# The state product of a chunked SSD scan as three products of split operands, with the state updated in place

## The chip, the cores and the metric

The kernel runs on one core of one Trainium2 chip. The metric is device time in microseconds of one execution. The kernel before took 1280.56 us, the median of three runs (1280.24 to 1281.42).

## The reference, cut to what matters

One decoder layer: a gated pooling branch beside a Mamba-2 state space branch, for a prompt of 1024 positions and for 8 short samples. The part that matters is the scan of the prompt. It goes over chunks of 128 positions; there are 32 heads of 64 channels in 4 groups, a state of 128 x 64 per head, and B and C are shared by the 8 heads of a group:

```python
def step(h, inp):
    xq, dq, Bq, Cq = inp
    acs = jnp.cumsum(dq * Ag, axis=1)
    ...
    y = jnp.einsum('bijge,bjgep->bigep', att, xq)
    y = y + jnp.einsum('bign,bige,bgepn->bigep', Cq, jnp.exp(acs), h)
    last = acs[:, -1]
    w_in = jnp.exp(last[:, None] - acs) * dq
    h = h * jnp.exp(last)[..., None, None] + jnp.einsum('bjgn,bjge,bjgep->bgepn', Bq, w_in, xq)
    return h, y
```

The last line but one is the state's update: the old state decayed, plus the product of B with x weighted by w_in. The change is about this line. All tensors are float32.

## The kernel before, in words

The kernel first normalises x, multiplies it with the input weights, and stores the branches' inputs in DRAM. Then comes a stretch in which TensorE (PE) alternates between two kinds of work, and in this stretch the change lies. At the end come the last group's output products, the product with w_o and the final norm.

**Two kinds of work.** One kind is 32 chunk rows, `seq`, each made by the generator `chunk(g, c)` for group g and chunk c. The other kind is blocks of output products (`gemm_`, L353 to L364, from `P_unit` and `S_unit`): 12 matmuls into one of three PSUM buffers (`psA`), in fp32r, a form of float32 in which the kernel multiplies split operands, a high half and a low half, as three products (L359 to L361). Such a block's result is taken from PSUM by ScalarE (ACT, L1741) or VectorE (DVE, L1723, L1744).

**The steps of a chunk row** are the stretches between the `yield` lines of `chunk`:

1. Loads by SP of the decays, B and C, and x (L1491 to L1497). x has five buffers, `xb`.
2. For c > 0 the factor cE of C, an exponential on ACT (L1501); the mask on GpSimd (POOL, L1192, called by `far`); eight exponentials on ACT (L1201, called by `exps`).
3. PE transposes x into the PSUM tile px and B into pbc, and multiplies B with C into pbc (L1510 to L1513). ACT copies B to `bt` (L1515) and C into pbc (L1517). DVE makes xd = x times dt (L1521) and xw = x times the weight (L1523, one buffer), and multiplies dec and cE with what stands in pbc (L1528, L1530).
4. The state product of bt and xw, a float32 matmul, into the single buffer of `psC` (L1535). Then `inner`: 16 products of xd and dec (L1213) and of the old state and cE (L1216) by head, in tiles of 64 columns. POOL decays the old state into a second buffer (L1541), DVE adds the product (L1543). DVE combines x and the inner products, four instructions (L1548), in place in x's buffer.
5. `finish` (L1468 to L1479): gate, split of the result, sum of squares. In the last chunk of a group a sixth step transposes the state (L1555) and stores it.

px, pbc and the result of `inner` take turns in the four PSUM buffers of `psB`.

**What sets the order.** A loop over i (L1807 to L1826) calls the steps of several rows in turn: step 3 of row i+1, some blocks of products, step 4 of row i, loads (step 1) of row i+3, step 2 of row i+2, step 5 of row i, more blocks. From i = 13 on, the split of w_o runs beside (`wo_splits`: ACT L1778, POOL L1780). PE and SP run the instructions in just the written order (`ORDER`, `in_line`). ACT, DVE and POOL each run their own in an order that a planner of the framework sets when the kernel is built, from its own costs and from the written order as the priority; on the chip each engine then works strictly in that order. Before the loop comes a prelude (L1799 to L1804) whose order is fixed on PE, ACT, DVE and SP.

Of the kernel before, what the change touches and what calls it, by code (L numbers as in the profile page):

```python
# [8 lines left out]
F32 = mybir.dt.float32  # L9
F32R = mybir.dt.float32r  # L10
AF = mybir.ActivationFunctionType
ALU = mybir.AluOpType
# [8 lines left out]
P = 128  # L21
# [25 lines left out]
def tile_pool_ssd_step(  # L47
# [6 lines left out]
    nc = tc.nc  # L54
    uid = [0]

    def nm(s):
        uid[0] += 1
        return f"{s}_{uid[0]}"
# [52 lines left out]
    mm = nc.tensor.matmul  # L112
    act = nc.scalar.activation
    V = nc.vector
# [1344 lines left out]
    hst = [None] * NG  # L1459
# [3 lines left out]
    def ckt(shape, tag, bufs=2):  # L1463
        return (cl if tag in CKL else ca if tag in ("dec", "xb", "cE", "bc") else ck).tile(list(shape), F32, tag=tag, name=nm(tag), bufs=bufs)
# [24 lines left out]
    def chunk(g, c):  # L1489
        o = c * P  # L1490
        dec = ckt([P, 8, P], "dec", 3)  # L1491
        decays(dec, g, c)
        bc = ckt([P, 2, P], "bc", 3)
        load(bc, xbc_d[g][:, 4:6, o:o + P])
        Bf, Cf = bc[:, 0], bc[:, 1]
        xb = ckt([P, 4, P], "xb", 5)
        load(xb, xbc_d[g][:, 0:4, o:o + P])  # L1497
        yield
        if c > 0:
            cE = ckt([P, 8, P], "cE")  # L1500
            act(cE, dec, AF.Exp, scale=-1.0)  # L1501
        if g > 0 or c > 0:
            far(dec, c)
            exps(dec, g, c)
            yield
        sz = ckt([P, 4, P], "sz", 3)
        load(sz, z_d[g][:, :, o:o + P])
        px = PB()
        for q in range(4):
            nc.tensor.transpose(px[:, q * P:(q + 1) * P], xb[:, q], ident)  # L1510
        pbc = PB()
        nc.tensor.transpose(pbc[:, :P], Bf, ident)
        mm(pbc[:, P:2 * P], Bf, Cf, start=True, stop=True)  # L1513
        bt = ckt([P, P], "bt", 2)
        act(bt, pbc[:, :P], AF.Copy)  # L1515
        if c > 0:
            act(pbc[:, 2 * P:3 * P], Cf, AF.Copy)  # L1517
        pxv = px.rearrange("p (h d) -> p h d", d=64)
        heads = slice(8 * g, 8 * g + 8)
        xd = ckt([P, 8, 64], "xd", 2)  # L1520
        V.tensor_tensor(xd, pxv, dtT[:, c, heads].unsqueeze(2).to_broadcast([P, 8, 64]), ALU.mult)  # L1521
        xw = ckt([P, 8, 64], "xw", 1)
        V.tensor_tensor(xw, pxv, wdT[:, c, heads].unsqueeze(2).to_broadcast([P, 8, 64]), ALU.mult)  # L1523
        if g == c == 0:
            yield
            far(dec, c)
            exps(dec, g, c)
        V.tensor_tensor(dec, dec, pbc[:, P:2 * P].unsqueeze(1).to_broadcast([P, 8, P]), ALU.mult)  # L1528
        if c > 0:
            V.tensor_tensor(cE, cE, pbc[:, 2 * P:3 * P].unsqueeze(1).to_broadcast([P, 8, P]), ALU.mult)  # L1530
        yield
        if c == 0:
            yh[g], yl[g] = [Y4(hs if g % 2 else hp) for _ in range(2)]
        pu = PC()
        mm(pu, bt, xw.rearrange("p h d -> p (h d)"), start=True, stop=True)  # L1535
        pi = inner(xd, dec, P, *((hst[g], cE) if c > 0 else ()))
        hn = ckt([P, 512], "hst", 2)
        if c == 0:
            act(hn, pu, AF.Copy)
        else:  # L1540
            nc.gpsimd.tensor_tensor(hn.rearrange("p (h d) -> p h d", d=64), hst[g].rearrange("p (h d) -> p h d", d=64),  # L1541
                                    Elb[:, c, heads].unsqueeze(2).to_broadcast([P, 8, 64]), ALU.mult)
            V.tensor_tensor(hn, hn, pu, ALU.add)  # L1543
        hst[g] = hn

        v = xb
        for q in range(4):
            V.scalar_tensor_tensor(v[:, q], v[:, q], Dv[:, 4 * g + q:4 * g + q + 1], pi[:, q], ALU.mult, ALU.add)  # L1548
        yield
        finish(g, o, P, v, sz)  # L1550
        if c == NC - 1:
            yield
            pt = PB()
            for q in range(4):
                nc.tensor.transpose(pt[:, q * P:(q + 1) * P], hn[:, q * P:(q + 1) * P], ident)  # L1555
            fo = ckt([P, 4, P], "xb", 5)
            act(fo, pt.rearrange("p (q n) -> p q n", n=P), AF.Copy)
            store_(new_ssm_p[0, 0, 8 * g:8 * g + 8].rearrange("(q h) p n -> (h p) q n", h=2), fo)
# [241 lines left out]
    for _ in range(FRONT - 1):  # L1800
        next(pc_)
    next(seq[0])
    next(seq[1])
    next(pc_)  # L1804
    in_line(first_engines)
    order = tuple(mybir.EngineType[e] for e in ORDER)
    for i in range(len(seq)):  # L1807
        if i + 1 < len(seq):
            next(seq[i + 1])
        products(i + 0.4)  # L1810
        if i > 0:
            next(seq[i - 1], None)
        next(seq[i], None)
        if i % NC == 2:
            ends = sample_end(i // NC)
            next(ends)
        if i + 3 < len(seq):
            next(seq[i + 3])
        if i + 2 < len(seq):
            next(seq[i + 2])  # L1820
        next(seq[i], None)
        if i % NC == 4:
            next(ends, None)
        if i > 12:
            next(wos, None)
        products(i + 1.0)  # L1826
# [229 lines left out]
```

## Time and profile before

| | |
|---|---|
| median of three runs | 1280.56 us (1280.24 to 1281.42) |
| profiled execution | 1284.38 us, span 1282.6 us |
| granted PE clock, mean | 0.996 |
| busy over the span | PE 98%, DVE 71%, ACT 51%, POOL 51% |
| first state product (L1535) | 830.8 us after the span's start |
| last state product | 1099.7 us |
| state products recorded | 64, two per call, mean 591 ns |

The span is what the profiler saw from the first to the last instruction; the execution's own time is 1.8 us longer. "PEld" rows are weight loads of PE, which overlap with its matmuls. In a row of instructions in order of time, the first number is the start in us, the second the duration, then the engine, the line, the operation and the tiles (output, arrow, inputs), the count, and in square brackets the idle time before with what ended it. The tiles ps and pc are PSUM buffers of psB and psC, and mm is one of psA. In the view of waits a row gives who waited for whom, the us in total, the number of times and the longest.

### The profile page before, as it was taken

How to read it: one execution, taken by the hardware profiler on the slowest of the kernel's cores; microseconds unless marked ns; L12 is line 12 of the kernel's file. 1: busy time of each engine (PE TensorE's matmuls, PEld its weight loads, DVE VectorE, ACT ScalarE, POOL GpSimd, SP SyncE). 2: the span in 40 equal slices, each digit the busy share in tenths (PEclk: the TensorE clock that was granted, in tenths of full speed). 3: DMA queues.
4: the chain of work that ended last, by engine and by line, in shares of the span. 5: the costliest groups of instructions: out<-in, count | busy, mean ns of one | idle time of the engine just before them, and what ended most of it. 6: DMA issues, size and time to landing. Idle time of an engine off the chain costs nothing.

```text
span 1282.6 us, 26320 instructions
## 1 busy us (share of the span) xinstructions
PE 1256.3 (98%) x9739; PEld 1170.9 (91%) x9739; DVE 911.9 (71%) x1635; ACT 654.9 (51%) x1508; POOL 653.9 (51%) x556
## 2 busy tenths in 40 slices
PE   7999999999999999999999999999999999999997
PEld 6779999989999999999999999989889889999786
DVE  4686678976989588676676765488667887579343
ACT  4665337465546645454655554655676756202111
POOL 1007659677868878555444444345666867300000
PEclk9999999999999999999999999999999999999999
DMA  9736354465456453444556564999779898675531
GB/s 331 243 119 215 123 165 154 152 208 171 143 164 212 152 161 124 165 154 121 171 173 197 170 187 147 331 306 305 231 221 278 271 295 266 211 265 180 212 107 50
DMA packets 232769, 251.68 MB, mean 196 GB/s; under 512 B 29729, under 2 KB 176881, under 8 KB 232634
## 3 DMA queue, kind: packets, MB, share of 16 engines
q1 hardware_dynamic: 160544, 171.60, 42.8%
q10 hardware_dynamic: 72098, 78.41, 17.8%
q8 instruction: 77, 1.26, 0.4%
q14 instruction: 50, 0.41, 0.1%
HBM read 167.06 MB, written 83.01 MB: 195 GB/s over the span
## 4 chain that ended last, share of the span: by engine, by line
PE 74%; issue 3%; DMA 2%; DVE 2%; POOL 2%; ACT 1%; ACTq 0%; SPq 0%; POOLq 0%; DVEq 0%
PE mm L359 7%; PE mm L360 6%; PE mm L361 6%; PE ps L608 6%; PE ps L609 6%; PE mm L608 6%; PE ps L610 6%; PE mm L610 6%; PE mm L609 6%; PE ps L1213 3%; PE ps L2002 2%; PE ps L2003 2%; PE ps L2004 2%; PE pc L1535 2%; PE ps L1216 2%
## 5 line engine op out<-in xcount | busy, mean ns | idle before, releaser
L168 POOL TENSOR_TENSOR wlo<-rawA,whi 128x512 fp32r<-128x512 f32 x120 | 180.3, 1506 | 169.5 <-ACT whi L165 90.1
L168 POOL TENSOR_TENSOR wlo<-raw,whi 128x512 fp32r<-128x512 f32 x92 | 148.7, 1623 | 124.0 <-ACT whi L165 111.2
L359 PE MATMUL mm<-Y,whi 128*128 128x352 f32 (+1 forms) x480 | 163.9, 342 | 0.0
L360 PE MATMUL mm<-Y,whi 128*128 128x352 f32 (+1 forms) x480 | 158.0, 329 | 0.3 <-DVE Y L1573 0.3
L361 PE MATMUL mm<-Y,wlo 128*128 128x352 f32 (+1 forms) x480 | 157.6, 328 | 0.0
L610 PE MATMUL mm<-Y,wlo 128*128 128x272 f32 x496 | 144.2, 291 | 4.5 <-POOL wlo L168 4.0
L608 PE MATMUL mm<-Y,whi 128*128 128x272 f32 x496 | 146.3, 295 | 0.6 <-DVE GA L624 0.5
L608 PE MATMUL ps<-Y,whi 128*128 128x272 f32 x496 | 143.6, 290 | 0.2 <-ACT o L1068 0.2
L609 PE MATMUL ps<-Y,whi 128*128 128x272 f32 x496 | 143.0, 288 | 0.0
L609 PE MATMUL mm<-Y,whi 128*128 128x272 f32 x496 | 142.6, 288 | 0.0
L610 PE MATMUL ps<-Y,wlo 128*128 128x272 f32 x496 | 142.6, 287 | 0.0
L1056 DVE SCALAR_TENSOR_TENSOR GA<-GA,cvT,GA 128x1112 f32<-128x1112 f32 x72 | 125.5, 1746 | 1.9 <-ACT GA L1053 1.8
L165 ACT ACTIVATE whi<-rawA 128x512 fp32r<-128x512 f32 x125 | 78.3, 627 | 92.7 <-PE ps L609 49.1
L165 ACT ACTIVATE whi<-raw 128x512 fp32r<-128x512 f32 x96 | 58.9, 627 | 108.0 <-DVE raw L554 51.0
L610 PEld LDWEIGHTS mm<-Y,wlo 128*128 128x128 f32 x496 | 93.4, 188 | 6.5 <-POOL wlo L168 5.4
L1201 ACT ACTIVATE dec<-dec,acT 128x128 f32<-128x128 f32 (+1 forms) x288 | 86.6, 383 | 22.7 <-POOL dec L1192 22.3
L608 PEld LDWEIGHTS mm<-Y,whi 128*128 128x128 f32 x496 | 93.3, 188 | 3.0 <-DVE GA L624 0.6
L359 PEld LDWEIGHTS mm<-Y,whi 128*128 128x128 f32 x480 | 90.8, 189 | 5.7 <-issue 4.3
L609 PEld LDWEIGHTS mm<-Y,whi 128*128 128x128 f32 x496 | 93.4, 188 | 0.9
L608 PEld LDWEIGHTS ps<-Y,whi 128*128 128x128 f32 x496 | 93.3, 188 | 0.7 <-ACT o L1068 0.4
L609 PEld LDWEIGHTS ps<-Y,whi 128*128 128x128 f32 x496 | 93.3, 188 | 0.2 <-issue 0.2
L610 PEld LDWEIGHTS ps<-Y,wlo 128*128 128x128 f32 x496 | 93.4, 188 | 0.0
(455 smaller groups left out, 3756.8 us busy)
## 6 DMA issues: line engine op xcount, KB each, us to landing
rawA<-in_w_in SPq DMA_DIRECT2D x46, 512.0 KB
dec<-acs_d SPq DMA_DIRECT2D x32, 512.0 KB
xbc<-GA ACTq DMA_DIRECT2D x24, 512.0 KB
rawA<-in_w_in SPq DMA_DIRECT2D x32, 256.0 KB
pw<-in_w_ssm_out ACTq DMA_DIRECT2D x32, 256.0 KB
ws<-ph ACTq DMA_DIRECT2D x32, 256.0 KB
ws<-pw SPq DMA_DIRECT2D x32, 256.0 KB
h<-in_state_ssm SPq DMA_DIRECT2D x32, 256.0 KB
```

Of the source, the lines that this page charges most:

```text
L165: ins = act(hi[:, :, :ncols], raw[:, :, :ncols], AF.Copy)
L168: (eng or nc.gpsimd).tensor_tensor(lo[:, :, :ncols], raw[:, :, :ncols], hi[:, :, :ncols].bitcast(F32), ALU.subtract)
L359: mm(ps[:, :n], a, rh[k][:, o:o + n], start=(k == 0), stop=False)
L360: mm(ps[:, :n], a, rl[k][:, o:o + n], start=False, stop=False)
L361: mm(ps[:, :n], b, rh[k][:, o:o + n], start=False, stop=(k == nk - 1))
L608: mm(p, hi, ah, start=(k == 0), stop=False)
L609: mm(p, hi, al, start=False, stop=False)
L610: mm(p, lo, ah, start=False, stop=(k == 3))
L1056: V.scalar_tensor_tensor(d[:, :n], rp[:, k:k + n], cvT[:, 24 * k + mc:24 * k + mc + 1], d[:, :n], ALU.mult, ALU.add)
L1201: act(dec[:, h], dec[:, h], AF.Exp, bias=acT[:S, c, 8 * g + h:8 * g + h + 1], scale=-1.0)
L1213: mm(o[hh], xd[:S, 2 * q + hh, :], dec[:S, 2 * q + hh], start=True, stop=state is None)
L1216: mm(o[hh], state[:, h * 64:h * 64 + 64], cE[:, h], start=False, stop=True)
```

## The change

The state product becomes three fp32r products: B's high half with xw's high half, B's low half with xw's high half, and B's high half with xw's low half. For that the row gets a new step between steps 3 and 4. In it ACT copies the high halves (of xw from px, of B from pbc), and DVE subtracts them to get the low halves. All four tiles have one buffer; `bt` had two. xw is no longer a tile of its own: the product with the weight is written back into px, which stays in use until the new step is done, as does pbc.

The loop calls the new step of row i+1 just after step 4 of row i; the prelude calls it for row 0.

The state has one buffer in place of two. POOL decays it in place, after the inner products have read it, and DVE's addition of the product is written behind the four instructions of L1548 instead of ahead of them. x keeps its five buffers.

```diff
         nc.tensor.transpose(pbc[:, :P], Bf, ident)
         mm(pbc[:, P:2 * P], Bf, Cf, start=True, stop=True)
-        bt = ckt([P, P], "bt", 2)
-        act(bt, pbc[:, :P], AF.Copy)
...
-        xw = ckt([P, 8, 64], "xw", 1)
-        V.tensor_tensor(xw, pxv, wdT[:, c, heads].unsqueeze(2).to_broadcast([P, 8, 64]), ALU.mult)
+        V.tensor_tensor(pxv, pxv, wdT[:, c, heads].unsqueeze(2).to_broadcast([P, 8, 64]), ALU.mult)
...
         yield
+
+        bth, btl = (ck.tile([P, P], F32R, tag=t, name=nm(t), bufs=1) for t in ("bt", "btl"))
+        xwh, xwl = (ck.tile([P, 512], F32R, tag=t, name=nm(t), bufs=1) for t in ("xw", "xwl"))
+        act(xwh, px, AF.Copy)
+        act(bth, pbc[:, :P], AF.Copy)
+        V.tensor_tensor(xwl, px, xwh.bitcast(F32), ALU.subtract)
+        V.tensor_tensor(btl, pbc[:, :P], bth.bitcast(F32), ALU.subtract)
+        yield
...
         pu = PC()
-        mm(pu, bt, xw.rearrange("p h d -> p (h d)"), start=True, stop=True)
+        mm(pu, bth, xwh, start=True, stop=False)
+        mm(pu, btl, xwh, start=False, stop=False)
+        mm(pu, bth, xwl, start=False, stop=True)
         pi = inner(xd, dec, P, *((hst[g], cE) if c > 0 else ()))
-        hn = ckt([P, 512], "hst", 2)
         if c == 0:
-            act(hn, pu, AF.Copy)
+            hst[g] = ckt([P, 512], "hst", 1)
+            act(hst[g], pu, AF.Copy)
         else:
-            nc.gpsimd.tensor_tensor(hn.rearrange("p (h d) -> p h d", d=64), hst[g].rearrange("p (h d) -> p h d", d=64),
-                                    Elb[:, c, heads].unsqueeze(2).to_broadcast([P, 8, 64]), ALU.mult)
-            V.tensor_tensor(hn, hn, pu, ALU.add)
-        hst[g] = hn
+            hv = hst[g].rearrange("p (h d) -> p h d", d=64)
+            nc.gpsimd.tensor_tensor(hv, hv, Elb[:, c, heads].unsqueeze(2).to_broadcast([P, 8, 64]), ALU.mult)
+        hn = hst[g]
...
         for q in range(4):
             V.scalar_tensor_tensor(v[:, q], v[:, q], Dv[:, 4 * g + q:4 * g + q + 1], pi[:, q], ALU.mult, ALU.add)
+        if c > 0:
+            V.tensor_tensor(hn, hn, pu, ALU.add)
         yield
...
     next(seq[0])
+    next(seq[0])
     next(seq[1])
...
         next(seq[i], None)
+        if i + 1 < len(seq):
+            next(seq[i + 1])
         if i % NC == 2:
```

## The prediction, made before the result was known

> **What bounds the kernel now.** I read three views in this order: the head of the page, the busy time of each engine in the stretches that hold the 32 chunk rows (four groups of eight), and TensorE's instructions in order of time inside one chunk row.
>
> ```profile
> span 1282.6 us, 26320 instructions
> PE 1256.3 (98%) x9739; PEld 1170.9 (91%) x9739; DVE 911.9 (71%) x1635; ACT 654.9 (51%) x1508; POOL 653.9 (51%) x556
> ...
> core 0: us, PE busy (x) PEld busy (x) DVE busy (x) ACT busy (x) POOL busy (x), PEclk, DMA share, GB/s
> 830.80:900.00 69.20, 69.20 (x558) 61.47 (x558) 54.86 (x98) 37.70 (x98) 36.15 (x41) 1.00 0.93 299
> 900.00:969.00 69.00, 69.00 (x557) 61.27 (x556) 47.93 (x79) 48.29 (x128) 43.32 (x52) 1.00 0.74 227
> 969.00:1039.90 70.90, 70.90 (x569) 63.22 (x568) 56.51 (x99) 46.20 (x119) 54.42 (x61) 1.00 0.91 287
> 1039.90:1108.50 68.60, 68.60 (x552) 61.05 (x551) 53.70 (x95) 37.53 (x93) 47.69 (x56) 1.00 0.76 235
> ```
>
> In the chunk stretch PE is busy for all of 277.7 us at a granted clock of 1.00. The 32 rows take about 8.7 us each. DVE is at 79%, 69%, 80% and 78% of the four groups, ACT at most at 70%, POOL at most at 77%. So what is taken from PE here is taken from the time, as long as the other engines keep up. Busy PE is modelled, so I look at starts:
>
> ```profile
> 908.57 1.02 PE L1535 MATMUL pc<-xw,bt 128*128 128x512 f32 x2
> 909.52 0.44 PE L1213 MATMUL ps<-dec,xd 128*64 128x128 f32 x4
> ...
> 911.10 0.39 PE L1216 MATMUL ps<-cE,hst 128*64 128x128 f32 x4
> ...
> 913.45 0.27 PE L1510 MATMUL ps<-ident,xb 128*128 128x128 f32 x1
> ...
> 1099.65 1.02 PE L1535 MATMUL pc<-xw,bt 128*128 128x512 f32 x2
> 1100.61 0.44 PE L1213 MATMUL ps<-dec,xd 128*64 128x128 f32 x4
> ```
>
> The state product (L1535) is one call recorded as two passes. From its start to the start of the inner products (L1213) it costs 0.95 us in an early row and 0.96 us in the last: there is no wait in it. That 0.95 us, 32 times, is what the change attacks.
>
> **What PE gains.** The new call is three products of 512 columns in fp32r. The nearest such products are in the kernel's tail:
>
> ```profile
> 1194.22 0.39 PE L2003 MATMUL ps<-Y,G 128*128 128x512 f32 x1
> 1194.45 0.40 PE L2004 MATMUL ps<-Y,G 128*128 128x512 f32 x1
> 1194.68 0.39 PE L2003 MATMUL ps<-Y,G 128*128 128x512 f32 x1
> ...
> 618.15 1.04 PE L1303 MATMUL ps<-ident,h 128*128 128x128 f32 x8
> 619.12 0.68 PE L1213 MATMUL ps<-dec,xd 64*64 64x64 f32 x16
> ...
> 905.87 0.60 PE L1510 MATMUL ps<-ident,xb 128*128 128x128 f32 x4
> 906.30 0.27 PE L1512 MATMUL ps<-ident,bc 128*128 128x128 f32 x1
> ```
>
> They start 0.23 us apart, so three take 0.69 us. The step to the 64 column tiles of L1213 has to be added. After eight transposes it shows by itself: four transposes take 0.43 us (905.87 to 906.30), eight 0.86, and L1213 starts 0.97 us after L1303, 0.11 later. I take 0.1 us after the new products too, 0.79 us in all. Each row saves 0.95 - 0.79 = 0.16 us, 32 rows **5.1 us**. No row shows a 64 column tile straight behind an fp32r product. If that step cost nothing, the saving is 0.26 us a row, 8.3 us; if it were twice as long, 0.06 us a row, 1.9 us.
>
> [...]
>
> **What the other engines get.**
>
> ```profile
> L1539 ACT ACTIVATE hst<-pc x4: 579/590/599, 831.9 to 1044.6; 128x512 f32<-128x512 f32 x4
> L1515 ACT ACTIVATE bt<-ps x32: 250/258/279, 818.8 to 1089.4; 128x128 f32<-128x128 f32 x32
> L1517 ACT ACTIVATE ps<-bc x28: 255/272/283, 829.9 to 1089.6; 128x128 f32<-128x128 f32 x28
> L1543 DVE TENSOR_TENSOR hst<-hst,pc x28: 670/677/690, 840.7 to 1100.8; 128x512 f32<-128x512 f32 x28
> L1548 DVE SCALAR_TENSOR_TENSOR xb<-xb,Dv,ps x128: 335/341/348, 834.7 to 1103.4; 128x128 f32<-128x128 f32 x128
> L1523 DVE TENSOR_TENSOR xw<-ps,wdT x32: 673/684/693, 820.3 to 1093.9; 128x512 f32<-128x512 f32 x32
> L1541 POOL TENSOR_TENSOR hst<-hst,Elb x28: 1039/1047/1544, 832.7 to 1097.6; 128x512 f32<-128x512 f32 x28
> ```
>
> ACT: the copy xwh is a new 512 column copy out of PSUM, 0.59 us like L1539. The copy of B stays one 128 column copy (0.26 us), now to fp32r. DVE: xwl is a 512 column operation on PSUM and SBUF, 0.68 us like L1543. For btl, 128 columns, I take 0.3 us, just under L1548's 0.34; even at 0.68 it changes only the load. The product with wdT now writes back into PSUM. No DVE row of this kernel does that. ACT pays 0.27 us into PSUM (L1517) against 0.26 out of it (L1515), so I leave 0.68 us; the bounds are 0.6 and 1.2 us. DVE thus gets 8 x 0.98 = 7.8 us more per group, against periods 1.3 us shorter: 62.7 of 67.9 us, 92%, then 82%, 92% and 91%. ACT gets 4.7 us, at most 53.0 of 67.7, 78%. POOL's decay is the same 1.05 us in place. No DMA is issued in the moved step, SP's queue keeps its order, and the new step in the prelude is ACT and DVE work before chunk 0's first product. All this costs **nothing as long as it hides under PE**; uncovered, the 0.98 us a row on DVE alone would be 31 us.
>
> **What is moved, and what is late next.**
>
> ```profile
> DVE dec L1528 <- ACT ps L1517: 20.7, 14, 3.1
> ...
> DVE xw L1523 <- PE pc L1535: 11.2, 12, 2.6
> ...
> DVE dec L1528 <- ACT bt L1515: 5.9, 3, 2.8
> ...
> 1027.67 1.21 DVE L1530 TENSOR_TENSOR cE<-cE,ps 128x1024 f32<-128x1024 f32 x1
> 1064.23 1.11 DVE L1548 SCALAR_TENSOR_TENSOR xb<-xb,Dv,ps 128x128 f32<-128x128 f32 x4
> 1072.02 1.21 DVE L1530 TENSOR_TENSOR cE<-cE,ps 128x1024 f32<-128x1024 f32 x1
> 1073.15 1.12 DVE L1548 SCALAR_TENSOR_TENSOR xb<-xb,Dv,ps 128x128 f32<-128x128 f32 x4
> 1089.34 1.21 DVE L1530 TENSOR_TENSOR cE<-cE,ps 128x1024 f32<-128x1024 f32 x1
> ...
> 1029.55 1.02 PE L1535 MATMUL pc<-xw,bt 128*128 128x512 f32 x2
> 1065.64 0.59 PE L1535 MATMUL pc<-xw,bt 128*128 128x512 f32 x1
> 1073.39 1.02 PE L1535 MATMUL pc<-xw,bt 128*128 128x512 f32 x2
> 1090.78 1.02 PE L1535 MATMUL pc<-xw,bt 128*128 128x512 f32 x2
> ```
>
> The wait of xw for the state product (11.2 us of DVE's idle time) goes, because the product no longer needs a single buffer. Its successor is xwh: single buffered, so it waits for the previous row's three products. From their old end (909.52) to the transposes that take over the PSUM slot (913.45 for the first) are 3.93 us; xwh and xwl need 0.59 + 0.68 and two hand-offs, some 1.5 us. That holds.
>
> Tighter is the copy of B. Today dec (L1528) waits for the copy L1515, though it reads other columns: accesses of ACT and DVE to one PSUM tile keep their written order. In the change the copy of B is written behind dec and cE (L1528, L1530), so B's halves are late by 0.26 + 0.3 us and a hand-off behind cE's end. Mostly cE ends some us ahead. But in the 20th to 31st rows, where w_o is split beside, it ends at 1073.23 for a product at 1073.39, and at 1090.55 for one at 1090.78. I charge 0.35 us for each of these two, **0.7 us**.
>
> [...]
>
> Sum: -5.1 + 0.7 = -4.4 us. The profiled execution took 1284.38 us (span 1282.6 and 1.8 around it), so it would be 1280.0. It is 3.8 us above the median of the three runs, 1280.56; the same difference on the median gives **1276.2 us**.
>
> **Rivals.**
>
> *The saving is eaten (about 1279.7).* The sum into the state and the next product share one PSUM buffer (psC has one). Today the decay runs a row ahead, and L1543 can follow the product at once. In place, the decay waits for the row's own inner products, and the addition is written behind the four L1548: 2.9 us from the product's start to the end of the inner products (908.57 to 911.49), decay 1.05, addition 0.68, with hand-offs about 5 of the 8.7 us of a row. DVE serves dec and cE first. In the late rows its order would then be cE, the L1548, the addition. With the rows above, the addition ends at 1074.9 for the product at 1073.39 (1.5 us late), at about 1092.2 for 1090.78 (1.4), at about 1030.5 for 1029.55 (1.0) and at about 1065.9 for 1065.64 (0.3): 4.2 us. Against: in most rows the room is larger, and an order made anew could put the addition ahead of dec while that waits for ACT.
>
> *DVE becomes the limit (slower, about 1285.3).* The same queue, with the new 0.98 us in front of the addition: the four late rows lose 0.9 us more each, and I add, as an estimate, 0.5 us for each of four rows that have a little more room: 4.2 + 3.6 + 2.0 = 9.8 us, net +4.7 us. It decides once more than about 5 us of waits appear on PE. For it: DVE at 92% in a strict order, with rows that have only 0.2 us left today. Against: 26.6 us of DVE's idle time are waits for L1517 and L1515, into which the new work can fall.
>
> *Three products are no cheaper (about 1278.6).* The doubled step gives -1.9 us. Only the size of the step speaks for it; the starts of the fp32r products are measured.
>
> **How the numbers follow.** A measurement of this kernel can tell 0.2%, 2.6 us, from no change. The forecast has 0.46, with the step's lower bound (1272.3) as its best case. The saving eaten and the products no cheaper have 0.22 together; both lie within 0.2%. DVE as the limit has 0.32. The range takes in the lower bound and the DVE case with some 3 us more, **1272.3 to 1288**; above lie some heavier pile-ups on DVE, below almost nothing.
>
> **What would show it.** Right: from the first state product to L1213's successor 0.79 us in every row, PE busy all through the four groups, and these some 5 us shorter together; DVE near 90% with shorter waits for ACT. Wrong: PE's weight loads waiting for the addition into the state, for btl or for the copy of B, in the rows beside the split of w_o above all; or the inner products waiting for the state. If the starts of the new products lie further apart than 0.23 us without a wait, the gain was mis-sized, not hidden. A changed order on ACT or POOL, say the decay behind a w_o split of 1.3 us, would make the prediction wrong by the same route.

## The result, and the profile after

The changed kernel took 1284.34 us, the median of 18 runs (1282.08 to 1287.68), against 1282.2 us for the kernel before in 18 runs beside them (1279.79 to 1287.97). The ratio is **1.0021, 95% interval 1.0011 to 1.0031**: slower, by about 2.7 us by the ratio and 2.1 us by the medians, where 4.4 us less were forecast. The profiled execution of the changed kernel took 1282.82 us.

That number must not be set against the 1284.38 us of the profiled execution before: there an earlier stage had run longer. The first transposes of the chunk rows came at 816.69 us in it and come at 814.41 us now. So I compare a **stretch**, from the first transposes of x (L1510) to the first matmul for the sums of squares (L1852 before, L1863 after), which every kernel here has. It takes 307.97 us before and 1124.70 - 814.41 = 310.29 us after: 2.32 us more, about the timed difference. Outside it the two profiled executions differ by 3.8 us the other way, in stages that the change does not touch: 2.3 us ahead of it and 1.5 us behind it, where the granted clock before was 0.57 from 1128 to 1132 us, and after it stayed at 1.00 from 1127 to 1132 us.

First the head of the page after, then the same four groups of rows as in the prediction (columns: PE, PEld, DVE, ACT, POOL, clock, DMA share, GB/s).

```profile
span 1281.1 us, 26491 instructions
...
PE 1251.9 (98%) x9771; PEld 1175.2 (92%) x9771; DVE 931.5 (73%) x1699; ACT 673.3 (53%) x1542; POOL 649.3 (51%) x556
```

```profile
830.00:900.00 70.00, 68.51 (x572) 62.80 (x568) 60.48 (x115) 44.78 (x118) 35.87 (x40) 1.00 0.93 300
900.00:969.00 69.00, 68.96 (x573) 63.67 (x570) 53.23 (x97) 53.46 (x140) 44.68 (x54) 1.00 0.76 232
969.00:1039.00 70.00, 69.40 (x576) 64.25 (x575) 62.99 (x114) 50.14 (x129) 53.10 (x61) 1.00 0.94 287
1039.00:1108.00 69.00, 65.92 (x537) 60.39 (x537) 55.79 (x108) 38.70 (x94) 45.36 (x55) 1.00 0.72 221
```

PE was busy for the whole of each group before. Now it is idle in each, most in the last, 3.1 of 69 us. The clock is 1.00 throughout, so the loss is waiting. DVE is at 86%, 77%, 90% and 81%.

The product itself, in an early row and in the last one, in order of time on PE:

```profile
907.25 0.39 PE L1540 MATMUL pc<-xw,bt 128*128 128x512 f32 x1
907.48 0.40 PE L1541 MATMUL pc<-xw,btl 128*128 128x512 f32 x1
907.72 0.40 PE L1542 MATMUL pc<-xwl,bt 128*128 128x512 f32 x1
908.04 0.44 PE L1213 MATMUL ps<-dec,xd 128*64 128x128 f32 x4
...
1099.85 0.39 PE L1540 MATMUL pc<-xw,bt 128*128 128x512 f32 x1
...
1100.64 0.44 PE L1213 MATMUL ps<-dec,xd 128*64 128x128 f32 x4
```

From the first product to the inner products are 0.79 us in both, as forecast: 0.23 + 0.24 and 0.32 for the last one with the step to 64 columns. The gain on PE is 32 x 0.16 = 5.1 us.

What took it back are waits of PE in the rows. In square brackets stand the idle time and what ended it:

```profile
833.69 0.30 PE L1512 MATMUL ps<-ident,bc 128*128 128x128 f32 x1 [0.56 <-DVE xb L1554]
853.73 0.47 PE L1540 MATMUL pc<-xw,bt 128*128 128x512 f32 x1 [0.50 <-DVE hst L1556]
886.10 0.30 PE L1512 MATMUL ps<-ident,bc 128*128 128x128 f32 x1 [0.43 <-PE ps L1510]
992.59 0.47 PE L1540 MATMUL pc<-xw,bt 128*128 128x512 f32 x1 [0.60 <-DVE hst L1556]
1061.08 0.33 PE L1512 MATMUL ps<-ident,bc 128*128 128x128 f32 x1 [0.60 <-DVE xwl L1534]
1064.31 0.47 PE L1540 MATMUL pc<-xw,bt 128*128 128x512 f32 x1 [0.75 <-ACT Y L1470]
1070.39 0.33 PE L1512 MATMUL ps<-ident,bc 128*128 128x128 f32 x1 [0.54 <-DVE xwl L1534]
1073.97 0.47 PE L1540 MATMUL pc<-xw,bt 128*128 128x512 f32 x1 [1.10 <-DVE hst L1556]
```

There are two kinds. The product (L1540) waits for the addition into the state (L1556), which has to empty the one buffer of psC; at 1064.31 too, where the profile names ACT's Y, the addition ends just ahead, at 1064.16. The transpose of B (L1512) waits for a PSUM slot, which xwl (L1534) or the combination with the inner products (L1554) still holds; for the one at 886.10 the profile names only PE's own transposes. To add them up I take, for each step from one PE instruction to the next in the stretch, what it exceeds the usual length of the same step by: 3.6 us before products, 3.0 us before transposes of B and 0.7 us in two odd places, **7.3 us**. Before, the same sum is 0.4 us. 307.97 - 5.1 + 6.9 = 309.8, against 310.29 measured.

The chain behind the worst of them, from DVE's, POOL's and ACT's instructions:

```profile
1067.38 1.22 DVE L1525 TENSOR_TENSOR dec<-dec,ps 128x1024 f32<-128x1024 f32 x1 [1.17 <-ACT dec L1201]
1068.52 1.22 DVE L1527 TENSOR_TENSOR cE<-cE,ps 128x1024 f32<-128x1024 f32 x1
...
1070.26 1.11 DVE L1554 SCALAR_TENSOR_TENSOR xb<-xb,Dv,ps 128x128 f32<-128x128 f32 x4
...
1073.14 0.68 DVE L1556 TENSOR_TENSOR hst<-hst,pc 128x512 f32<-128x512 f32 x1
```

```profile
1067.88 1.30 POOL L1788 TENSOR_TENSOR pw<-pw,ph 128x512 fp32r<-128x512 f32 x1 [0.69 <-ACT ph L1786]
...
1069.41 1.05 POOL L1549 TENSOR_TENSOR hst<-hst,Elb 128x512 f32<-128x512 f32 x1
```

The inner products that read the state end at about 1067.1 on PE. The decay, in place, could start then; it stands on POOL behind the low half of w_o (L1788), which itself waited for ACT, and starts at 1069.41. It is over at 1070.46, though, and is not what comes last. That is DVE: from dec at 1067.38, which had waited 1.17 us for ACT, DVE runs without a gap, and the addition has its place behind cE, xwl, L1554 and four more. It ends at 1073.8; PE wanted the buffer at about 1072.7.

The other three late products (853.73, 992.59 and 1064.31) are alike. The decay was over 3.5, 1.4 and 3.4 us before the addition began, DVE had no gap just before the addition, and a little earlier it had stood 2.72, 0.53 and 1.43 us for a load of a sample's rows (v). btl stands between DVE's wait and the addition in all four rows, xwl in two. So what makes the addition late in the changed kernel is its place in DVE's order, behind a wait of DVE for a load or for ACT, and not the decay on POOL.

### The profile page after: what moved, and what is told of

Read it like the earlier page. It is cut to its first block, busy times and chain, and to the rows that moved or that the text cites. A ratio compares the mean times of both kernels' runs of the same rounds, so it can differ in the third digit from the quotient of the medians.

```text
span 1281.1 us, 26491 instructions
## 1 busy us (share of the span) xinstructions
PE 1251.9 (98%) x9771; PEld 1175.2 (92%) x9771; DVE 931.5 (73%) x1699; ACT 673.3 (53%) x1542; POOL 649.3 (51%) x556
## 4 chain that ended last, share of the span: by engine, by line
PE 74%; DMA 9%; DVE 5%; issue 5%; ACT 3%; POOL 3%; SPq 1%; ACTq 1%; POOLq 0%; DVEq 0%
PE ps L608 6%; PE mm L608 6%; PE ps L609 6%; PE ps L610 6%; PE mm L610 6%; PE mm L609 6%; PE mm L359 5%; PE mm L360 5%; PE mm L361 5%; PE ps L2013 2%; PE ps L1213 2%; PE ps L2014 2%; PE ps L2015 2%; PE ps L233 2%; PE ps L1216 2%
```

## The experiments

The stretch and PE's waits in it, from one profile of each kernel, beside the timed ratio to the kernel before:

| kernel | stretch us | waits us | ratio, 95% interval |
|---|---|---|---|
| before | 307.97 | 0.4 | 1 |
| after | 310.29 | 7.3 | 1.0021, 1.0011 to 1.0031 |
| c_inplace_only | 314.49 | 6.5 | 1.0051, 1.0038 to 1.0064 |
| a_two_states | 311.95 | 7.9 | 1.0037, 1.0023 to 1.0051 |
| n_no_low | 310.41 | 7.4 | 1.0026, 1.0016 to 1.0036 |
| f_prio | 310.97 | 7.5 | 1.0015, 1.0007 to 1.0024 |
| g_early | 315.03 | 11.9 | 1.0046, 1.0032 to 1.0060 |
| q_wo_behind | 312.72 | 8.5 | 1.0045, 1.0032 to 1.0057 |
| gq | 309.05 | 5.0 | 1.0014, 1.0005 to 1.0022 |
| h_no_wo | 307.39 | 4.0 | one run |
| p_pw2 | 311.24 | 3.6 | 1.0019, 1.0010 to 1.0028 |
| pq | 307.96 | 0.4 | 0.9998, 0.9990 to 1.0007 |
| ag | 313.36 | 10.5 | 1.0050, 1.0036 to 1.0063 |
| agq | 323.01 | 16.9 | 1.0104, 1.0087 to 1.0122 |
| agw | 334.26 | 25.5 | 1.0224, 1.0207 to 1.0240 |
| gl | 321.50 | 18.1 | 1.0064, 1.0050 to 1.0078 |
| glq | 306.74 | 4.1 | 1.0000, 0.9991 to 1.0008 |
| bh | 309.06 | 1.4 | 1.0108, 1.0092 to 1.0124 |
| gh | 306.69 | 3.9 | 1.0071, 1.0057 to 1.0085 |
| agh | 304.28 | 1.8 | 1.0073, 1.0058 to 1.0087 |

Where the three products are, the stretch without waits is 308 - 5.1 = 303 us, and 303 plus the waits gives the measured stretch within 1.5 us up to 12 us of waits; with the float32 product it is 308. Steps at a lower clock count as waits here too: the stretch has one period of 3.4 us at a granted clock of 0.50 in n_no_low, a_two_states and ag, four in gl and agq and five in agw, and none in the others. The one in n_no_low cost 1.7 us (rows in the last section). In gl the granted clock is 0.95 in each of the last two groups of rows, in ag 0.98 in the third; over the whole profiled execution it is 0.996 in a_two_states, 0.993 in agq and 0.991 in agw, against 0.998 after. A profile is of one execution, so where two kernels lie close the ratio decides.

**The theories.** One: the state in one buffer, decayed in place and added to late, ties product, inner products, decay, addition and the next product into one chain, and PE waits at its end. Two: the added 0.97 us of DVE a row is too much for it. Three: the added step holds px and pbc too long. Four, formed after the first runs: the waits start where the split of w_o blocks ACT's and POOL's queues for a late load.

### The two halves of the change

**c_inplace_only**: the kernel before, with only the handling of the state changed: one buffer, the decay in place, and the addition behind the four instructions of L1548.

```diff
-        hn = ckt([P, 512], "hst", 2)
+            hst[g] = ckt([P, 512], "hst", 1)
...
-            V.tensor_tensor(hn, hn, pu, ALU.add)
+        if c > 0:
+            V.tensor_tensor(hn, hn, pu, ALU.add)
```

> The kernel before with only the state's part of the change: one state buffer, decayed in place, the addition written behind the four L1548; the state product stays one float32 call of 0.95 us. Theory 1 (the state's addition comes late for the one accumulator): PE waits for the addition in some four rows, 3 to 4 us in all, and the time is 3 to 4 us above before. Theory 2 (DVE's added load makes everything late): DVE has no added load here, so PE waits less than 1 us and the time is within 1 us of before. Theory 3 (px and pbc hold their PSUM slots too long): they are held as before, so no wait and no difference.

1286.77 us, against 1280.8 us before on the same chip. The single float32 product is still there, so nothing is gained, and the stretch grows by 6.5 us, 6.0 of it waits. The largest, on PE and on DVE:

```profile
1066.22 1.10 PE L1535 MATMUL pc<-xw,bt 128*128 128x512 f32 x2 [2.72 <-ACT Y L1470]
```

```profile
1059.65 1.47 DVE L1468 TENSOR_TENSOR v<-v,szs 128x256 f32<-128x256 f32 x1 [4.20 <-DMA v<-ys]
1061.04 1.21 DVE L1528 TENSOR_TENSOR dec<-dec,ps 128x1024 f32<-128x1024 f32 x1
...
1065.40 0.67 DVE L1549 TENSOR_TENSOR hst<-hst,pc 128x512 f32<-128x512 f32 x1
```

The profile names ACT's Y as the releaser, but that does not touch the buffer; DVE's addition ends at 1066.07, just ahead of the product. Follow DVE back: it stood 4.20 us at the head of its queue for a load of a sample's rows (v). The kernel before has the same kind of wait (two, 4.0 us in all, the longer 2.7) and PE doesn't notice, since there the addition needs no inner product and stands ahead of the four L1548. **Theory one is shown** as far as the handling of the state goes: without any split product it costs 6 us by itself, more than the 3 to 4 expected. Not every link of the chain is shown. The decay was over at 1062.02 here, and the addition waited for its place on DVE; whether the single buffer is needed for the loss, or the later place of the addition is enough, no run separates.

**a_two_states**: the change with the state's old handling; to make room in SBUF, w_o's split gets two raw buffers in place of three, with the store of the low half issued half a row earlier.

> The changed kernel with the state's old handling: two state buffers, decay a row ahead, addition straight behind the product. The room comes from the split of w_o, which gets two buffers instead of three, with its store issued earlier in the row. Theory 1: the waits for the addition, 3.6 us in the changed kernel's trace, are gone, some 3 us of slot waits stay, and the time is 2 us below before. Theory 2: DVE is as loaded as in the changed kernel, PE's waits keep their sum of 6 us in other places, and the time is at or just above before. Theory 3: only slot waits, 3 us, time 2 us below before.

1286.18 us. No product waits for the addition any more, but transposes wait, the largest of them:

```profile
1007.99 0.30 PE L1512 MATMUL ps<-ident,bc 128*128 128x128 f32 x1 [1.00 <-PE ps L1510]
...
1042.91 0.55 PE L1510 MATMUL ps<-ident,xb 128*128 128x128 f32 x3 [1.28 <-ACT xb L1564]
...
1072.57 0.45 PE L1512 MATMUL ps<-ident,bc 128*128 128x128 f32 x1 [2.21 <-issue]
```

At 1072.57 the slot had come free with xwl, which DVE ran from 1071.78 to 1072.47. So slots held until xwl do make PE wait, as theory three has it. The outcome as a whole, waits at other places and a time above before, is the one that had been written down for theory two. How much of the 1.0037 is the room made for it is settled by the control **p_pw2**, the kernel before with that edit alone:

```diff
                 load(at(n - 2, 1), raws.pop(n - 2))
+            yield
...
-                raws[n] = ck.tile([P, 512], F32, tag="pw", name=nm("pw"), bufs=3)
+                raws[n] = ck.tile([P, 512], F32, tag="pw", name=nm("pw"), bufs=2)
...
+        if i > 12:
+            next(wos, None)
         products(i + 0.4)
```

> The kernel before with only the buffers of w_o's split changed as in the kernels with two states (two raw buffers in place of three, the store of the low half issued half a row earlier). Control: if that change is harmless, it is the same as before within 0.1%; if it costs some 1 to 2 us, then the two-state kernel's 1.0037 holds that much that has nothing to do with the products.

1.0019: one buffer fewer for w_o, with the earlier store, costs the kernel before some 2.4 us, with two waits of 1.17 and 1.73 us for DVE's cE. So, if the two losses add, about half of a_two_states's is not the change's, and the kernels ag, agq and agw below, which need this room too, carry a handicap. It also shows a rival that stands beside all the theories: the planner makes a new order for every kernel, and an edit to a side job alone moved the time by 2.4 us. A difference of that size between two kernels needs a wait in the trace to say what it comes from.

### The load on DVE, and the planner's priorities

**n_no_low**: the change without the two subtractions on DVE.

```diff
-        V.tensor_tensor(xwl, px, xwh.bitcast(F32), ALU.subtract)
-        V.tensor_tensor(btl, pbc[:, :P], bth.bitcast(F32), ALU.subtract)
...
-        mm(pu, btl, xwh, start=False, stop=False)
-        mm(pu, bth, xwl, start=False, stop=True)
+        mm(pu, bth, xwh, start=False, stop=False)
+        mm(pu, bth, xwh, start=False, stop=True)
```

> The changed kernel without the low halves: the two DVE subtractions are left out (0.97 us a row), and the three products use the high halves each time, so the state is not the reference's. PE's cost is still 0.79 us a row, 5.1 us less than before. Theory 1: the waits for the addition stay, 3 to 4 us, and the time is 1 to 2 us below before. Theory 2: the waits are gone and the time is about 5 us below before. Theory 3: waits of PE's transposes for the slots stay, now for the copy of xw, 2 to 3 us, and the time is 2 to 3 us below before; with theories 1 and 3 together it is at before.

1284.1 us, 1.0026: no gain at all from 0.97 us a row less on DVE, where theory two expected 5 us. **So theory two, that the load is too much in itself, falls**, though not cleanly: the order of the engines is a new one, and up to 1.7 us of the 7.4 is the period at a clock of 0.50. The longest wait is seen whole on ACT, POOL, DVE and PE:

```profile
1050.98 0.63 ACT L1784 ACTIVATE ph<-pw 128x512 fp32r<-128x512 f32 x1 [4.36 <-DMA pw<-in_w_o]
```

```profile
1051.69 1.28 POOL L1786 TENSOR_TENSOR pw<-pw,ph 128x512 fp32r<-128x512 f32 x1 [7.82 <-ACT ph L1784]
1052.93 1.04 POOL L1547 TENSOR_TENSOR hst<-hst,Elb 128x512 f32<-128x512 f32 x1
```

```profile
1054.00 0.69 DVE L1554 TENSOR_TENSOR hst<-hst,pc 128x512 f32<-128x512 f32 x1 [3.65 <-POOL hst L1547]
```

```profile
1054.84 0.47 PE L1538 MATMUL pc<-xw,bt 128*128 128x512 f32 x1 [2.30 <-DVE hst L1554]
```

A piece of w_o lands late; ACT's high half of it (L1784) is next in ACT's queue and waits; POOL's low half is next in POOL's queue and waits for ACT; the decay stands behind that, the addition behind the decay, the product behind the addition. DVE stood idle for 3.65 us of it. In the kernel before, the same copy waited once for 5.2 us and PE did not wait for it. In the other long wait of this kernel, 2.05 us at 992.02, the decay was over at 988.79, and the addition, from 991.20, stood on DVE behind a wait of 1.27 us for v, as in the change.

**f_prio**: the change, with the decay, the addition and the new step raised in the planner's order.

```diff
+        with tc.high_priority(400):
+            act(xwh, px, AF.Copy)
...
+            with tc.high_priority(400):
+                nc.gpsimd.tensor_tensor(hv, hv, ...)
...
+            with tc.high_priority(400):
+                V.tensor_tensor(hn, hn, pu, ALU.add)
```

> The changed kernel with the decay, the addition and the four instructions of the new step given a higher priority when the order of ACT, DVE and POOL is made; nothing else changes. Theories 1 and 3: the late instructions come earlier in the queues, PE's 6 us of waits mostly go, and the time is 3 to 5 us below before. Theory 2: DVE's load is the same, what is put first delays dec, cE and the evacuations instead, and the time stays within 1 us of the changed kernel, 2 to 3 us above before.

1282.49 us, 1.0015. Its interval overlaps that of the change; a priority does not mend it. The addition for the product at 1075.50 still stands on DVE behind the four combining instructions and the same four others, so its place was not moved there, and the run does not tell the theories apart.

### The added step, and w_o's place in the queues

**g_early**: the change with the new step taken into step 3, right behind the product with the weight and ahead of dec and cE, so that px and pbc come free early; the loop is as before.

```diff
         V.tensor_tensor(pxv, pxv, wdT[...], ALU.mult)
+        act(xwh, px, AF.Copy)
+        act(bth, pbc[:, :P], AF.Copy)
+        V.tensor_tensor(xwl, px, xwh.bitcast(F32), ALU.subtract)
+        V.tensor_tensor(btl, pbc[:, :P], bth.bitcast(F32), ALU.subtract)
...
-        if i + 1 < len(seq):
-            next(seq[i + 1])
```

**q_wo_behind**: the change, with each step of w_o's split kept behind the last work of the row on ACT and POOL. **gq**: both. **pq**: the kernel before with that queueing.

```diff
         if i > 12:
-            next(wos, None)
+            with behind(mybir.EngineType.Activation), behind(mybir.EngineType.Pool):
+                next(wos, None)
```

> The changed kernel with the four splitting instructions back in step 3, written between the weighting of x and the products dec and cE; no new step. The state stays in place. If the slots of px and pbc are what is late (DVE makes xwl only after dec and cE), the transposes no longer wait, 3 of the 7 us of waits go and the time is at before or up to 1 us below. If it is the addition into the state, its 4 us of waits stay and nothing is gained where DVE now waits for the row's old product in front of dec: 1 to 3 us above before.

> The changed kernel with each step of the w_o split queued on ACT and POOL behind the instructions written before it (those of the row's last step), so that its waits for the loads do not stand in front of them. Theory A: the waits of the last two groups mostly go, 2 to 3 us in the first group stay, and the time is 2 to 3 us below before. Theory B: no change against the changed kernel, 2 to 3 us above before.

> Both edits of the two kernels before this one together. If the slots and the w_o pieces are the causes, next to no waits are left and the time is 4 to 5 us below before. If the state in place is the cause, waits for the addition stay, 3 us or more, and the time is within 2 us of before.

> The kernel before with each step of w_o's split queued behind the last work of the row on ACT and POOL, nothing else. If w_o's split is a trouble only for the recurrence through the single state buffer, this is the same as before within 0.1%. If the queueing itself moves things, it shows here.

g_early alone is worse, 1286.89 us: the steps before its transposes lose 1.6 us in place of 3.0, as theory three has it, but those before its products 8.8 in place of 3.6. q_wo_behind is worse too, 1286.55 us; the two together take 1282.68 us and have 5.0 us of waits in place of 11.9. pq is at 0.9998: the queueing costs the kernel before nothing. The waits of g_early, and that of gq for the same thing (total us, times, longest):

```profile
POOL pw L1786 <- ACT ph L1784: 16.7, 9, 5.6
ACT ph L1784 <- DMA wo<-ph: 8.4, 3, 3.7
PE pc L1538 <- DVE hst L1554: 7.5, 7, 2.0
ACT ph L1784 <- DMA pw<-in_w_o: 7.0, 4, 3.7
```

```profile
PE pc L1538 <- DVE hst L1554: 2.3, 4, 1.5
```

g_early's w_o copy waits 15.4 us for transfers at the head of ACT's queue; in gq no such wait is left, and PE's waits for the addition fall from 7.5 to 2.3 us. Work and traffic are the same in both: **the order of the queues does it**. The way from the copy to PE is not POOL's decay here. In g_early's longest wait, before the product at 992.05, the copy had waited 1.15 us for its load, xw's high half stood behind it on ACT, DVE waited 1.97 us for that with xwl, and the addition came behind xwl, with the decay over 2.7 us before.

By the expectation above, gq's remaining waits before products, 3.1 us, speak for the state in place. q_wo_behind without the early split gains nothing: its products still lose 4.6 us and its transposes 3.1 (1.76 in one of them). This fits the trace of the change, where none of the four late additions had waited for ACT's or POOL's part of the split. So theory four is seen at work in n_no_low and in the kernels with the early split; in the changed kernel itself the late loads that count are DVE's loads of v.

### No split of w_o beside the rows

**h_no_wo** is the change, **bh** the kernel before, **gh** g_early, and **agh** g_early with the state in two buffers, each with w_o copied unsplit to its place ahead of the rows and no split beside them.

```diff
+            for k in range(8):
+                for part in range(2):
+                    load(wo_d[k][:, part], w_o[0, k * P:(k + 1) * P, :])
...
-        if i > 12:
-            next(wos, None)
```

> The changed kernel without the split of w_o beside the last 19 rows: w_o is copied unsplit in DRAM in an earlier stage, so the output's last product is not the reference's, and the earlier stage carries 8 MB more of DMA. Only the stretch from the first transposes of the chunk rows to the row sums after them is compared (307.97 us before, 310.29 changed). Theory A (ACT's and POOL's queues stand still behind the w_o pieces that wait for their loads, and that makes the late instructions of the rows late): PE's waits after the 13th row go, 2 to 3 us of waits in the first group stay, and the stretch is 305 to 306 us. Theory B (the longer chain itself is too long for a row): waits of 4 us and more stay in the last two groups and the stretch is 308 us or more.

> The kernel before with no split of w_o beside the rows: w_o is copied unsplit to both halves' place in DRAM ahead of the rows, so the low half isn't formed, and the run has about 8 MB of traffic more at an earlier place. Control for the next two: the stretch from the first transposes to the row sums should stay at 308 us, because in the kernel before PE doesn't wait there at all. Its whole time is what the other two are measured against.

> The change with the split of B and xw at the end of step 3 instead of in a step of its own, and with no split of w_o beside the rows (copied unsplit ahead, as in the control). If the waits need w_o's split, the addition into the single state is in time in nearly every row: stretch 303 to 304 us, 4 to 5 us under its control. If the single state is too tight by itself, 2 us or more of waits for the addition stay and the stretch is 305 us or more.

> As the one above, with the state in two buffers and the addition early. If w_o's split is what starts the waits of the two-state kernel, no wait over 0.5 us is left: stretch 303 us, 5 us under the control, the full gain predicted for PE. If the added work on ACT and DVE is itself what is too much, waits for the low and high halves stay and the stretch is 305 us or more.

The extra copy makes all four slower as a whole, so gh and agh are compared with bh, on the same chip: bh 1294.96 us (1291.44 to 1296.16), **gh 1289.29** (1288.31 to 1290.09), **agh 1289.51** (1288.25 to 1290.51). That is 5.7 and 5.5 us less, and the ranges don't touch. Of the difference between the profiled executions (5.6 and 5.2 us) the stretch has 2.4 us in gh and 4.8 us in agh; the rest lies outside it and is not the products'. The third group of rows in bh, in gh and in agh:

```profile
983.00:1052.00 69.00, 69.00 (x550) 61.50 (x550) 55.63 (x98) 39.47 (x103) 40.01 (x49) 1.00 0.64 190
```

```profile
983.00:1052.00 69.00, 68.52 (x570) 63.36 (x569) 60.55 (x114) 45.58 (x120) 42.83 (x54) 1.00 0.64 190
```

```profile
983.00:1052.00 69.00, 69.00 (x577) 64.08 (x576) 60.71 (x113) 44.51 (x118) 42.94 (x52) 1.00 0.65 195
```

In agh PE is busy without a gap from 836 us to the end of the rows, with DVE at 88% of this group, doing all of the change's added work. In gh 1.5 us of waits remain in the rows, the longest of them 0.65 us before a product that waits for the addition. h_no_wo (one run, 1293.09 us), with the added step where the change has it, keeps 4.0 us, 2.7 of them before transposes of B, and its stretch of 307.39 us lies between the two forecasts. So without w_o beside them, with two states and the early split, the products bring nearly the 5 us that PE saves; with w_o they don't. These runs take away the split's work and its traffic together (DMA share 0.64 in gh in place of 0.92 after, from 983 to 1052 us); that order alone matters is shown by gq.

### Trying to keep both

**ag** is g_early with two states as in a_two_states (and p_pw2's edit), **agq** that with w_o queued behind as in gq. **agw** is ag with w_o in pieces of 256 columns, loaded one and a half rows ahead:

```diff
-                raws[n] = ck.tile([P, 512], F32, tag="pw", name=nm("pw"), bufs=2)
+                raws[n] = ck.tile([P, 256], F32, tag="pw", name=nm("pw"), bufs=5)
```

**gl** is g_early with ACT's and POOL's part of w_o half a row later, in a call of its own at the top of the loop, and **glq** that with this part queued behind the row's work (the line with behind is glq's).

```diff
         if i + 1 < len(seq):
             next(seq[i + 1])
+        if i > 13:
+            with behind(mybir.EngineType.Activation), behind(mybir.EngineType.Pool):
+                next(wos, None)
         products(i + 0.4)
```

> The three products, but the state in two buffers with the old early addition, and the split of B and xw made at the end of step 3, ahead of dec and cE, with no step of its own (w_o's split has two raw buffers, its store issued earlier). If the two costs seen so far, the addition into the single state and the long hold of px and pbc, are all there is against the products, both classes of PE waits vanish: stretch 308.0 - 5.1 = 303 us or a little more, about 0.4% faster than before (0.996). If the work on ACT and DVE for the low halves is itself too much, the waits come back at other places and it is no faster than the kernel before.

> As the one above, with each step of w_o's split queued behind the last work of the row on ACT and on POOL. If the late loads of w_o at the head of ACT's and POOL's queues still start waits, this one is 1 to 2 us faster than without it; if only the state and the slots mattered, the two are the same within 0.1%. Best case 303 us of stretch and 0.996 of the time before.

> A full kernel: three products, state in two buffers, early split, and w_o's split in pieces of 256 columns instead of 512, loaded one and a half rows ahead instead of one (five buffers of half the size). If late loads of w_o at the head of ACT's queue are the cause, the waits mostly go: stretch 303 to 305 us and 0.996 to 0.998 of the time before. If instead the number of small transfers and steps costs as much (twice as many on SP, ACT and POOL), it is 1.002 or more.

> The change with the split of B and xw at the end of step 3, and with ACT's and POOL's part of w_o's split written half a row later than its load allowed before (one and a half rows from load to use, still three buffers); the planner may still pull it forward. If the load's lateness is the cause and the order is kept, waits fall from 11.9 us to 3 us or less: stretch 303 to 306 us, 0.996 to 0.998 of before. If the planner pulls it forward again, the waits for the load and the addition stay and it is 1.002 or more.

> As the one above, with that part also queued behind the split of B and xw of the row on ACT and behind the row's last work on POOL, so that it can't be pulled forward. If a late load at the head of the queues is the cause: no wait of ACT for that load, stretch 303 to 305 us, 0.996 to 0.997 of before, faster than both kernels. If the amount of work beside the rows (ACT 0.6 and POOL 1.3 us a row) is the cause, 2 us or more of waits for the addition stay.

ag misses: 1287.32 us. Its two buffers for w_o make ACT wait 15.0 us for the loads, and the copy of B for the product behind that (2.42 us at 1026.82). agq is worse, 1295.9 us: SP runs in the written order, and the store of w_o's low half now waits on SP for POOL's later work (SP issues nothing from 1060.96 to 1070.22 us, then this store, and the load of x at 1073.23), so that loads of x are issued late and PE waits 4.04 us for one at 1079.77. agw, 1307.27 us, has twice the steps on every queue; its largest wait is 3.54 us. It says nothing on the cause. gl misses as well, 1289.64 us: the planner pulled the copy forward again and ACT waits 17.4 us for transfers of or around w_o. glq does what was meant with the queue. The waits of ACT's copy for transfers and of PE for the addition, in gl and in glq:

```profile
PE pc L1538 <- DVE hst L1554: 8.8, 6, 2.0
ACT ph L1788 <- DMA whi<-ws: 6.5, 1, 6.5
ACT ph L1788 <- DMA pw<-in_w_o: 6.3, 4, 2.8
ACT ph L1788 <- DMA wo<-ph: 4.6, 2, 2.5
```

```profile
PE pc L1538 <- DVE hst L1554: 1.2, 3, 0.6
ACT ph L1788 <- DMA wo<-ph: 1.0, 2, 0.7
```

ACT's waits fall from 17.4 to 1.0 us and PE's for the addition from 8.8 to 1.2 us. The kernel takes 1281.35 us against 1281.32 us before, 1.0000, where 0.996 to 0.997 had been expected: better than the change, but the 4.1 us of waits that are left and the 5.1 us gained are the same within the measurement. No kernel with the three products and all of the other work was faster than the one before.

## Why the prediction was wrong

**What PE gains** was right: 0.79 us from product to inner products, 0.16 us a row, 5.1 us. The rival of three products no cheaper is out. The durations taken over hold too: xwl 0.69 us (0.68 taken), the product written back into PSUM 0.69 us (0.68), btl 0.28 us (0.3).

**The step that failed** is the one on what is moved and what is late next, which charges 0.7 us for waits where the trace has 6.9 us more than before. It erred in two places.

- Of the new tiles and of the PSUM slots it said "That holds", from one early row with 3.93 us to spare. In rows whose DVE is late, xwl and L1554 free the slots behind the transposes: 3.0 us in the change, and a_two_states shows them without the in-place state.
- The addition behind the four L1548 was worked out, but set aside as a rival with the counter-argument that in most rows the room is larger. It is larger; but the room was what let late loads pass without harm: 3.6 us of waits before products in the change. c_inplace_only, 1.0051, shows that the new handling of the state alone costs more than the products bring.

The charge that was made, for the copy of B behind dec and cE, named a real wait: ACT's high half of B waits ten times, 10.7 us in all, for DVE's cE. No wait of PE in the list above is put down to it.

**The rivals.** "The saving is eaten" had the right mechanism, the addition late in DVE's order behind cE and L1548, and nearly its price: 3.6 us of waits for the addition where 4.2 were worked out. It had two of the four late rows right (those at 1064.31 and 1073.97); the products at about 1030 and 1091 did not wait, so that the sums agree is partly luck. It lacked the slots and the waits for v. "DVE becomes the limit" gave 1285.3 us, the nearest to the time, by 9.8 us of waits before products where 3.6 were measured, so its nearness is luck. Its reason is borne out in part: btl, and in two of the rows xwl, do stand ahead of the late addition. That the load as such is the limit is not borne out: n_no_low takes the 0.97 us a row away and gains nothing, and agh does this work without a wait in the rows. The sign that the prediction named last, the decay behind a w_o split of 1.3 us, is seen in n_no_low (1.28 us, at 1051.69), but in the change no product waited for it.

**What ties it together** is that PE at 100% hid how much of the other engines' slack was in use. ACT, POOL and DVE run in a fixed order, and in the kernel before, too, each of them stood for some us at the head of its queue for a late transfer, POOL by way of ACT:

```profile
POOL pw L1780 <- ACT ph L1778: 8.7, 7, 4.1
...
ACT ph L1778 <- DMA whi<-ws: 5.2, 1, 5.2
...
DVE v L1468 <- DMA v<-ys: 4.0, 2, 2.7
```

The old order, with two states and the addition free of the inner products, absorbed that. In n_no_low the decay at 1052.93 had no need of w_o's low half, but stood behind it on POOL, where that had waited 7.82 us for ACT.

**Open**: whether the later place of the addition would cost as much with two states, how much of each kernel's time is the planner's new order, why w_o's queueing helps only together with the early split, and how the split's work and its traffic share the effect.

## What to carry to other kernels

Before a buffer that decouples two engines is given up, look at the longest wait for a transfer at the head of each queue involved, not at the mean load: the buffer has to cover that wait even if no time is lost to it now (for v it was 2.7 us in the kernel before, where PE did not wait, and 4.20 us in c_inplace_only, where PE waited 2.72). A gain on the busiest engine is only as large as the slack that its suppliers keep once it runs faster: here PE gained 5.1 us and had 6.9 us of waits more. And a side job with loads of its own, queued among the work of a recurrence, can pass a late load on to it by the queues of ACT and POOL (n_no_low: 4.36 us on ACT, 2.30 us on PE), or hold back its loads on SP by a store (agq: 4.04 us on PE): moving it gained 4 us from g_early to gq, and nothing in the change as it stood.

## What the runs showed of the hardware

In n_no_low a wait of PE cost more than its length. After the wait of 2.30 us, in stretches of 1 us (PE clock in the third column from the right):

```profile
1056.00:1057.00 1.00, 1.00 (x18) 1.00 (x16) 0.32 (x1) 1.00 (x5) 0.72 (x2) 0.63 1.16 339
1057.00:1058.00 1.00, 1.00 (x12) 1.00 (x11) 0.40 (x1) 1.00 (x4) 0.00 (x0) 0.50 0.65 162
1058.00:1059.00 1.00, 1.00 (x11) 0.67 (x8) 1.00 (x2) 1.00 (x4) 0.91 (x1) 0.50 0.12 32
1059.00:1060.00 1.00, 1.00 (x4) 1.00 (x5) 1.00 (x2) 1.00 (x3) 1.00 (x2) 0.67 0.41 143
```

The granted clock falls to 0.50 at about 1056.3, 1.4 us after PE has started again at 1054.84, and stays there for about 3.4 us. The four shares of the clock are 1.70 us short of 4 us at 1.00, with PE busy all the time, so some 1.7 us are lost. In gl it falls too, after a wait of 2.03 us before the product at 991.78: it is 0.52, 0.50, 0.50 and 0.77 in the four microseconds from 993 on, and the steps of the inner products from 993.64 to 995.35 are 0.43 us long, in place of 0.22 from 1021.33 to 1022.42. Such steps of 0.43 us follow gl's waits of 1.96, 1.70 and 1.65 us before the products at 1029.75, 1059.73 and 1080.28 as well; the last has a further wait of 0.41 us behind it.

It does not follow every such wait: after the 2.72 us of c_inplace_only the clock stays at 1.00 in every microsecond from 1066 to 1073, and after the 1.73 us in p_pw2 from 1044 to 1048. So the length of the wait alone does not decide it; what does, these runs do not show.
